# A two-layer decoder trunk on one core: more products inside the opening's five steps, and eight weight tiles kept back at the end

## The chip, the core and the metric

The kernel runs on one core of a Trainium2 chip. The metric is device time in microseconds of one execution; the number for a kernel is the median of its runs. The engines are named as in the profile: PE is TensorE's matmuls and PEld its weight loads, DVE is VectorE, ACT is ScalarE, POOL is GpSimd, SP issues nearly all the DMAs.

## The reference

256 tokens of width 2048 go through two layers. Layer 0 mixes tokens with forgetting attention (16 heads of 128), layer 1 with sliding-window attention; each is followed by a gated feed-forward network with a short convolution. Every sub-layer is modulated by a conditioning vector `c`:

```python
def reference(x, c, positions, ...):
    c_act = jax.nn.silu(c)
    for i in range(DEPTH):
        mod = c_act @ ada_w[i] + ada_b[i]
        sh1, sc1, g1, sh2, sc2, g2 = jnp.split(mod[:, None, :], 6, axis=-1)
        h = x * (1.0 + sc1) + sh1
        ...
        y = fox_attention(h, fox_w_in[j], fox_b_f[j], fox_w_o[j])      # layer 0; layer 1: swa_attention
        x = layer_norm(DEEPNORM_ALPHA * x + (1.0 + g1) * y, ln_mix_g[i], ln_mix_b[i])
        h = x * (1.0 + sc2) + sh2
        y = conv_ffn(h, ffn_w_up[i], ffn_conv_w[i], ffn_conv_b[i], ffn_w_down[i])
        x = layer_norm(DEEPNORM_ALPHA * x + (1.0 + g2) * y, ln_ffn_g[i], ln_ffn_b[i])
    return x
```

All is in float32. So `h`, the input of the very first projection (2048 to 6144 columns for queries, keys and values), needs the shift `sh1` and the scale `1 + sc1` first, which are products of `c` with 33.5 MB of `ada_w`.

## The kernel before

**Products in three parts.** A float32 product is made of float32r products: every operand is split into a high half (`h`, `hH`, a cast on ACT) and a low half (`l`, `hL`, the rest, a subtraction on DVE), and three matmuls add high x high, high x low and low x high in PSUM.

**Units.** `stream` (line 260) fetches weights in tiles of 256 rows x 512 columns (512 KB), which are called units here. For each, SP issues a DMA into one of ten `w` buffers (line 265), ACT makes `wh` (line 268), DVE makes `wl` (line 279), and PE does 24 matmuls over 256 columns (`w_mm`, weights stationary) or 12 over 512 columns (`x_mm`, activations stationary). `wh` and `wl` have four buffers each. The whole kernel has 728 units. Work is kept in a list and emitted up to two units behind the fetches (`then`, `settle`, `rest`); the low half of a unit is emitted ahead of the unit's products.

**The opening** (`opening`, line 535) works on `sh1` and `sc1` in five steps, because 2048 columns of each come in pieces of 256, 256, 512, 512 and 512. In a step, pieces of `ada_w` (`wo`) arrive, DVE adds them up weighted by `c` (line 576, one sum for each 512 KB or less), a few matmuls of one column sum over the partitions (`products`, `totals`, tile `cps`), and the columns of `hH` and `hL` that the step makes known are written by `mod_pair`. With these the projection can begin before the rest of `h` exists: a list `plan` (line 898) says which units are done while each following step's pieces arrive. An entry `(blk, k2)` stands for three units (queries, keys and values of a block of four heads) at rows `256 * k2` to `256 * k2 + 255`. The first list is empty, and the sixth is what follows the steps. At the end of each step two units of the next list are emitted ahead of the step's transposes.

Four blocks of heads exist. A block that is not finished within the opening leaves partial sums in PSUM, which `keep` copies with ACT to SBUF (line 919; two tiles of 128x512 each for queries, keys and values), as the eight PSUM banks are wanted by the next. Some go to the four quarters of the tile `gate`, the others to tiles of the pool `gp`. Later, when the rest of the block's units is done, `evac_qk` (line 847) and `evac_v` (line 834) add them in with DVE (lines 852 and 838). Once the block whose sums lie in `gate` has read them, `gate_free` is set.

**After the opening** the blocks are finished in the order 0, 2, 1, 3: first what is left of the units of queries, keys and values of a block, then its four heads (scores, softmax, output) as background generators that advance with each unit. `out_proj` (line 750) multiplies the heads' outputs with `w_o`, 32 units: the first two column blocks go over heads 0 to 7, then 8 to 11, then 12 to 15, the other two over all at once. Each column block ends with a residual addition and statistics for the layer norm on DVE (`residual`, line 629).

**The modulation of what follows** is streamed beside this. `ada_vector` (line 373) makes one of the other modulation vectors: 32 tiles `wa` of 512 KB and for each a sum on DVE (lines 395 and 397), then a few more generator steps. How fast it goes is set by hand: `ada["rate"]` is the number of generator steps per unit, 1.6 for the rest of the opening's list, then 1.6, 1.6, 1.5 and 1.4 for the four blocks, then 1.3 in the output projection. Three vectors (119 steps, 96 sums) have to be ready by the end of the output projection. The sums and many other DVE instructions are kept in program order; the rest is ordered when the program is built.

**The end.** The feed-forward network of layer 1 ends with the down-projection's second part, ten units for each of four column blocks (`x_stationary`, line 323). For the last column block `x_mm_end` (line 298) does the last four units in two passes: first the products of token tile 0 of all four, then those of token tile 1. Token tile 0's chain (residual, statistics, the layer norm at lines 1180 and 1181, the output's DMAs) can so begin while PE does the second pass. The `wh` and `wl` of the units kept this way stay occupied until then.

Of the kernel before, what the change touches and what calls it, by code (L numbers as in the profile page):

```python
# [41 lines left out]
def hybrid_trunk(ctx: ExitStack, tc: tile.TileContext, a: dict, out: bass.AP):  # L42
# [217 lines left out]
    def stream(wsrc, row0, col, ks, use):  # L260

        for kc in ks[::2]:
            r0 = (row0 + kc) * P
            w = wtile()
            pin(nc.sync.dma_start(w, wsrc[r0:r0 + 2 * P, col:col + WB].rearrange("(k p) f -> p k f", p=P)), False)
            h = hl.tile([P, 2, WB], F32R, tag="wh", name="wh")
            l = hl.tile([P, 2, WB], F32R, tag="wl", name="wl")
            pin(nc.scalar.copy(h, w), False)  # L268

            def go(kc=kc, h=h, l=l):  # L270
                ahead[0] -= 1
                run_post()
                use(kc, h, l)
                if feeds:
                    feeds.pop(0)()
                tick()

            def residual_(w=w, h=h, l=l, go=go):
                pin(nc.vector.tensor_tensor(l, w, f32(h), op=ALU.subtract), behind[0] > 0)  # L279
# [470 lines left out]
    def out_proj(oT, full, w_o, l):  # L750
# [26 lines left out]
    def fox(l, j):  # L777
# [56 lines left out]
        def evac_v(ps, V, then, old):  # L834
# [8 lines left out]
            if old and old is next(iter(olds.values()))[2]:  # L843
                ada["gate_free"] = True
# [17 lines left out]
        def head(blk, hh, q, k, V):  # L862
# [22 lines left out]
            def outputs(pT):  # L885
# [15 lines left out]
        last = {}  # L901
        for items in plan:
            for blk, k2 in items:
                last[blk] = 2 * k2 + 1

        final = plan[-1][-1][0]

        def keep(blk, part):

            ps = banks[blk][part]  # L910
            if not old and part == 0:
# [3 lines left out]
                ada["gate_free"] = False  # L915
            g = [room.pop(0) if room else f32(gtile("part")).rearrange("p a b -> p (a b)") for _ in range(2)]
            old.setdefault(blk, []).append(g)
            for gi, pi in zip(g, ps):
                pin(nc.scalar.copy(gi, pi if part == 2 else pi.rearrange("p a s -> p (a s)")))
# [3 lines left out]
        def first_block(blk, k2, part):  # L923
            ps = banks.setdefault(blk, [None] * 3)
            k = 2 * k2
            if not done.get((blk, part)):
                then(lambda: ps.__setitem__(part, (w_banks, w_banks, x_banks)[part]()))

            def use(kc, h, l):
                if part < 2:  # L930
                    w_mm(ps[part], kc, h, l, last[blk])
                else:
                    x_mm(ps[part], kc, h, l, hstat, last[blk])
# [3 lines left out]
            if blk != final and k + 1 == last[blk]:  # L937
                then(lambda: keep(blk, part))
# [4 lines left out]
        for blk, rate in zip((0, 2, 1, 3), (1.6, 1.6, 1.5, 1.4)):  # L943
# [4 lines left out]
            def more(part, banks_, mul):  # L948
                if n == KC:
                    return banks[blk][part]  # L950
# [135 lines left out]
    def conv_ffn(l):  # L1086
# [37 lines left out]
        for si, (b0, b1) in enumerate(sbs):  # L1124
# [21 lines left out]
            for d in range(D // WB):  # L1146
                ps = x_stationary(w_dn, d * WB, b0 * 4, (b1 - b0) * 4, stat, (2, 4)[l] if si > 0 and d == D // WB - 1 else 0)
# [61 lines left out]
```

## Time and profile before

| | before |
|---|---|
| median of 3 runs | 2212.91 us (2211.6 to 2215.46) |
| the profiled execution | 2215.89 us, span 2214.0 us |
| units | 728 |
| units in the opening's five steps | 39, and 6 after them |
| last matmul of the kernel starts | 2199.79 us |
| last DVE instruction starts | 2208.82 us (a pair, 1.41 us) |

The prediction quotes views of one profiled execution. Times are microseconds from the span's start. A row of groups gives the line of the code, the engine, the operation, the tiles out<-in with their shapes, the count, then the busy time, the mean of one in nanoseconds, and the idle time before them. A row of waits gives who waited for whom, the sum, the number of waits and the longest. A row of windows gives the stretch and its length, the busy time and number of instructions of each engine, the granted clock of TensorE (1.00 is full), the DMA engines' share and what they moved. A row of the timeline gives start, duration, engine, line and instruction, with the idle time before it and what ended that in square brackets.

### The profile page before, as it was taken

To read this page: it belongs to the slowest core of one execution; us is meant where nothing else is said; L and a number is where in the kernel's file an instruction comes from. 1 tells how busy PE (TensorE), PEld (TensorE's weight loads), DVE (VectorE), ACT (ScalarE), POOL (GpSimd) and SP (SyncE) were. 2 spreads that over 40 slices of the span, in tenths; PEclk is the share of its full clock that TensorE was granted. 3 is DMA by queue.
4 is the path that set the end of the run, shared out by engine and by line. 5 is a ranking of instruction groups with operands and counts; after the bars stand their busy time and mean duration, and the time that the engine had idled before them with its cause. 6 is when DMAs were issued, how large, how long until landed. Compare 5 with 4: busy or idle time off the path is not lost. (4 is left out here: it accounts for less than half of the span.)

```text
span 2214.0 us, 38357 instructions
## 1 busy us (share of the span) xinstructions
PE 2164.3 (98%) x14915; PEld 1976.7 (89%) x14915; DVE 1792.8 (81%) x2459; ACT 1159.6 (52%) x1841; POOL 19.0 (1%) x48
## 2 busy tenths in 40 slices
PE   6999999999999999999999999999999999999997
PEld 5999888789999988999987877789999988999986
DVE  6879998989978979799798888789888655666756
ACT  3435656465565543655644677555555533555532
POOL 0000000000000000000000000000000000000000
PEclk9999999999999999999999999999999999999999
DMA  9999998979978989899797676678888566666663
GB/s 334 368 352 366 351 352 298 327 257 323 349 234 300 322 312 385 260 311 322 251 354 290 201 240 206 208 257 295 281 264 270 187 194 195 192 195 195 191 195 108
DMA packets 274246, 602.98 MB, mean 272 GB/s; under 512 B 21062, under 2 KB 29960, under 8 KB 273552
## 3 DMA queue, kind: packets, MB, share of 16 engines
q1 hardware_dynamic: 273008, 595.85, 79.6%
q0 software_dynamic: 1056, 4.69, 0.6%
q8 instruction: 116, 1.90, 0.3%
q14 instruction: 66, 0.54, 0.1%
HBM read 598.37 MB, written 2.10 MB: 271 GB/s over the span
## 5 line engine op out<-in xcount | busy, mean ns | idle before, releaser
L268 ACT CAST wh<-w 128x1024 fp32r<-128x1024 f32 x728 | 765.3, 1053 | 790.0 <-PE ws L75 284.5
L75 PE MATMUL ws<-hH,wh 128*128 128x256 f32 x6656 | 1153.3, 278 | 4.6 <-ACT hH L84 2.1
L279 DVE TENSOR_TENSOR wl<-w,wh 128x1024 fp32r<-128x1024 f32 x728 | 887.6, 1222 | 325.3 <-ACT wh L268 308.5
L75 PEld LDWEIGHTS ws<-hH,wh 128*128 128x128 f32 x6656 | 1012.1, 189 | 9.0 <-ACT hH L84 2.3
L75 PE MATMUL ws<-hH,wl 128*128 128x256 f32 x3328 | 918.6, 277 | 4.3 <-DVE wl L279 4.0
L75 PEld LDWEIGHTS ws<-hH,wl 128*128 128x128 f32 x3328 | 628.5, 189 | 6.0 <-DVE wl L279 5.9
L75 PE MATMUL xs<-wh,gT 128*128 128x512 f32 x1408 | 435.3, 389 | 0.0
L75 PEld LDWEIGHTS xs<-wh,gT 128*128 128x128 f32 x1408 | 264.3, 188 | 54.7
L75 PE MATMUL xs<-wl,gT 128*128 128x512 f32 x704 | 273.9, 389 | 0.0
L75 PE MATMUL xs<-wh,hH 128*128 128x512 f32 x704 | 235.9, 401 | 0.0
L397 DVE SCALAR_TENSOR_TENSOR acc<-wa,cact,acc 128x1024 f32<-128x1024 f32 x180 | 228.4, 1278 | 0.0
L397 DVE SCALAR_TENSOR_TENSOR acc<-wa,cactp,acc 128x1024 f32<-128x1024 f32 x128 | 162.3, 1278 | 0.3 <-DMA acc<-in_ada_b_dram 0.3
L75 PEld LDWEIGHTS xs<-wh,hH 128*128 128x128 f32 x704 | 131.3, 188 | 29.4 <-issue 0.7
L75 PEld LDWEIGHTS xs<-wl,gT 128*128 128x128 f32 x704 | 132.2, 188 | 27.4
L75 PE MATMUL xs<-wl,hH 128*128 128x512 f32 x352 | 138.7, 395 | 2.5 <-DVE wl L279 2.5
L1093 ACT ACTIVATE u<-ws,ccol 128x256 f32<-128x256 f32 x176 | 96.7, 562 | 58.5 <-PE ws L75 43.3
L75 PE MATMUL xs<-wh,oT 128*128 128x512 f32 x384 | 126.2, 397 | 0.8 <-ACT oT L84 0.8
L1094 DVE SCALAR_TENSOR_TENSOR u<-ws,ccol,u 128x255 f32<-128x255 f32 x176 | 82.6, 477 | 14.9 <-ACT u L1093 14.7
L75 PEld LDWEIGHTS xs<-wh,oT 128*128 128x128 f32 x384 | 72.1, 188 | 16.6 <-ACT oT L84 1.2
L1096 DVE SCALAR_TENSOR_TENSOR u<-ws,ccol,u 128x254 f32<-128x254 f32 x176 | 83.1, 477 | 2.2
L75 PEld LDWEIGHTS xs<-wl,hH 128*128 128x128 f32 x352 | 66.5, 189 | 17.5 <-DVE wl L279 4.3
L576 DVE SCALAR_TENSOR_TENSOR oacc<-wo,cact,oacc 128x1024 f32<-128x1024 f32 (+1 forms) x68 | 73.3, 1078 | 8.3 <-DMA wo<-in_ada_w_dram 7.1
(220 smaller groups left out, 1280.4 us busy)
## 6 DMA issues: line engine op xcount, KB each, us to landing
w<-in_ffn_w_up_dram SPq DMA_DIRECT2D x352, 512.0 KB, 4.7
wa<-in_ada_w_dram SPq DMA_DIRECT2D x320, 512.0 KB, 5.6
w<-in_ffn_w_down_dram SPq DMA_DIRECT2D x176, 512.0 KB, 4.9
w<-in_fox_w_in_dram SPq DMA_DIRECT2D x96, 512.0 KB, 6.9
wo<-in_ada_w_dram SPq DMA_DIRECT2D x48, 512.0 KB, 9.0
w<-in_swa_w_in_dram SPq DMA_DIRECT2D x40, 512.0 KB, 4.6
w<-in_fox_w_o_dram SPq DMA_DIRECT2D x32, 512.0 KB, 6.2
w<-in_swa_w_o_dram SPq DMA_DIRECT2D x32, 512.0 KB, 4.8
```

The source lines that it names most:

```text
L75: return nc.tensor.matmul(o, lhsT, rhs, start=start, stop=stop, **kw)
L268: pin(nc.scalar.copy(h, w), False)
L279: pin(nc.vector.tensor_tensor(l, w, f32(h), op=ALU.subtract), behind[0] > 0)
L397: pin(nc.vector.scalar_tensor_tensor(ac, wo, (cactp if row else cact)[:, k:k + 1], ac, op0=ALU.mult, op1=ALU.add), True)
L576: nc.vector.scalar_tensor_tensor(acc, w[:, k], cact[:, kc:kc + 1], acc, op0=ALU.mult, op1=ALU.add)
L1093: nc.scalar.activation(u, pf, AF.Identity, bias=cw(CW, f), scale=cw(2, f))
L1094: nc.vector.scalar_tensor_tensor(u[:, 1:], pf[:, :S - 1], cw(1, f), u[:, 1:], op0=ALU.mult, op1=ALU.add)
L1096: nc.vector.scalar_tensor_tensor(u[:, 2:], pf[:, :S - 2], cw(0, f), u[:, 2:], op0=ALU.mult, op1=ALU.add)
```

## The change

Three things are changed.

1. The plan. Before, the block visits in the opening were 2 (one entry), 1 (two), 3 (four), 0 (eight). Now they are 3 (one), 1 (two), 2 (four), 3 again (five), 0 (eight). The units in the five steps go from 0 + 6 + 9 + 12 + 12 = 39 to 0 + 6 + 9 + 15 + 18 = 48, and those after them from 6 to 12. `keep` is called for four visits of three parts; where a block already has partial sums, DVE adds the PSUM tile to them instead of ACT copying it. The gate tile's quarters go to block 1, which is the first whose sums are read.
2. The rest of the blocks is finished in the order 0, 1, 2, 3, with 0, 18, 12 and 6 units left (before, for 0, 2, 1, 3: 0, 21, 18 and 12). The rates of ada steps are 1.6, 1.6, 1.6 and 1.5 for the blocks and 1.5 in layer 0's output projection.
3. The last column block of layer 1's down-projection keeps eight units instead of four for the second pass. The first four of these have `wh` and `wl` in the space of `hH` and `hL`, whose last use is past, the other four in the four buffers.

```diff
-    def stream(wsrc, row0, col, ks, use):
+    def stream(wsrc, row0, col, ks, use, spare={}):
...
-            h = hl.tile([P, 2, WB], F32R, tag="wh", name="wh")
-            l = hl.tile([P, 2, WB], F32R, tag="wl", name="wl")
+            h, l = spare.get(kc) or (hl.tile([P, 2, WB], F32R, tag=n, name=n) for n in ("wh", "wl"))
...
+    def spares(nk):
+        t = [hpad[:, 56 + i * 2 * WB:56 + (i + 1) * 2 * WB].rearrange("p (a f) -> p a f", a=2) for i in range(8)]
+        return {nk - 16 + 2 * i: (t[2 * i], t[2 * i + 1]) for i in range(4)}
...
-        stream(wsrc, k0, col, list(range(nk)), use)
+        stream(wsrc, k0, col, list(range(nk)), use, spares(nk) if end == 8 else {})
...
-            then(lambda i=i: ada.update(rate=(1.3, 0.65)[l]))
+            then(lambda i=i: ada.update(rate=(1.5, 0.65)[l]))
...
-        then(lambda: (ada_need(l, 2), ada.update(rate=(1.3, 0.75)[l])))
+        then(lambda: (ada_need(l, 2), ada.update(rate=(1.5, 0.75)[l])))
...
-            if old and old is next(iter(olds.values()))[2]:
+            if old and old is olds[1][2]:
                 ada["gate_free"] = True
...
-        plan = [[], [(2, 0), (1, 0)], [(1, 1), (3, 0), (3, 1)], [(3, 2), (3, 3), (0, 0), (0, 1)],
-                [(0, 2), (0, 3), (0, 4), (0, 5)], [(0, 6), (0, 7)]]
+        plan = [[], [(3, 0), (1, 0)], [(1, 1), (2, 0), (2, 1)], [(2, 2), (2, 3), (3, 1), (3, 2), (3, 3)],
+                [(3, 4), (3, 5), (0, 0), (0, 1), (0, 2), (0, 3)], [(0, 4), (0, 5), (0, 6), (0, 7)]]
...
+        visits = []
         for items in plan:
             for blk, k2 in items:
-                last[blk] = 2 * k2 + 1
+                if not visits or visits[-1][0] != blk:
+                    visits.append((blk, []))
+                visits[-1][1].append(k2)
+        visit = {(blk, k2): (n, 2 * ks[0], 2 * ks[-1] + 1) for n, (blk, ks) in enumerate(visits) for k2 in ks}
+        first_read = 1
...
+            parts = old.setdefault(blk, [])
+            flat = [pi if part == 2 else pi.rearrange("p a s -> p (a s)") for pi in ps]
+            if part < len(parts):
+                for gi, pi in zip(parts[part], flat):
+                    nc.vector.tensor_tensor(gi, pi, gi, op=ALU.add)
+                return
             g = [room.pop(0) if room else f32(gtile("part")).rearrange("p a b -> p (a b)") for _ in range(2)]
-            old.setdefault(blk, []).append(g)
-            for gi, pi in zip(g, ps):
-                pin(nc.scalar.copy(gi, pi if part == 2 else pi.rearrange("p a s -> p (a s)")))
+            parts.append(g)
+            for gi, pi in zip(g, flat):
+                pin(nc.scalar.copy(gi, pi))
...
-            if blk != final and k + 1 == last[blk]:
-                then(lambda: keep(blk, part))
+            if k + 1 == v1:
+                if v1 < KC - 1:
+                    then(lambda: keep(blk, part, ps[part]))
+                else:
+                    banks[blk, part] = ps
...
-        for blk, rate in zip((0, 2, 1, 3), (1.6, 1.6, 1.5, 1.4)):
+        for blk, rate in zip((0, 1, 2, 3), (1.6, 1.6, 1.6, 1.5)):
...
-                ps = x_stationary(w_dn, d * WB, b0 * 4, (b1 - b0) * 4, stat, (2, 4)[l] if si > 0 and d == D // WB - 1 else 0)
+                ps = x_stationary(w_dn, d * WB, b0 * 4, (b1 - b0) * 4, stat, (2, 8)[l] if si > 0 and d == D // WB - 1 else 0)
```

More of the change, by code (lines that the diff above doesn't have):

```diff
@@ L896, in fox, with keep @@
         TC = KC // 2
-        plan = [[], [(2, 0), (1, 0)], [(1, 1), (3, 0), (3, 1)], [(3, 2), (3, 3), (0, 0), (0, 1)],
-                [(0, 2), (0, 3), (0, 4), (0, 5)], [(0, 6), (0, 7)]]
+        plan = [[], [(3, 0), (1, 0)], [(1, 1), (2, 0), (2, 1)], [(2, 2), (2, 3), (3, 1), (3, 2), (3, 3)],
+                [(3, 4), (3, 5), (0, 0), (0, 1), (0, 2), (0, 3)], [(0, 4), (0, 5), (0, 6), (0, 7)]]
         done, banks, old = {}, {}, olds
-        last = {}
+        visits = []
         for items in plan:
             for blk, k2 in items:
-                last[blk] = 2 * k2 + 1
[L906 to L911, printed above, removed]
+                if not visits or visits[-1][0] != blk:
[3 more added lines that the diff above has]
+        first_read = 1
+        def keep(blk, part, ps):
+            if blk == first_read and part == 0:
                 gt = cst.tile([P, D], F32, tag="gate", name="gpart")
@@ L915, in keep @@
                 ada["gate_free"] = False
+            parts = old.setdefault(blk, [])
[4 more added lines that the diff above has]
+                return
             g = [room.pop(0) if room else f32(gtile("part")).rearrange("p a b -> p (a b)") for _ in range(2)]
[L917 to L919 removed]
+            parts.append(g)
+            for gi, pi in zip(g, flat):
+                pin(nc.scalar.copy(gi, pi))
         room = []
         def first_block(blk, k2, part):
[L924 removed]
+            n, v0, v1 = visit[blk, k2]
+            ps = banks.setdefault(n, [None] * 3)
             k = 2 * k2
[L926 removed]
+            if k == v0:
                 then(lambda: ps.__setitem__(part, (w_banks, w_banks, x_banks)[part]()))
@@ L946, in fox, with more @@
             n = done.get((blk, 0), 0)
-            def more(part, banks_, mul):
+            def more(part, banks_, mul, n=n, blk=blk):
                 if n == KC:
-                    return banks[blk][part]
+                    return banks[blk, part][part]
                 ps = banks_()
```

4 lines of the change are left out of this document (2 added, 2 removed).

## The prediction

> **What bounds the kernel now.** I read the page first, for the engines' shares.
>
> ```profile
> span 2214.0 us, 38357 instructions
> PE 2164.3 (98%) x14915; PEld 1976.7 (89%) x14915; DVE 1792.8 (81%) x2459; ACT 1159.6 (52%) x1841; POOL 19.0 (1%) x48
> ```
>
> PE (TensorE) is busy almost throughout, so only places where it waits can give time back. Next comes the view of windows, from step 3 of the opening up to the last unit of the output projection. A unit is one 512 KB weight tile with its products: 24 matmuls over 256 columns or 12 over 512. The windows begin where the timeline, with matmuls counted, shows a unit's first one. Columns: window, its length, busy us (instructions) of PE, PEld, DVE, ACT, POOL, clock, DMA share, GB/s.
>
> ```profile
> 86.90:126.50 39.60, 39.60 (x279) 37.24 (x278) 34.02 (x34) 17.89 (x23) 0.00 (x0) 0.94 1.02 364
> 126.50:170.00 43.50, 42.93 (x298) 39.50 (x297) 35.40 (x36) 15.23 (x17) 2.58 (x5) 0.96 0.99 337
> 170.00:187.60 17.60, 16.92 (x122) 15.42 (x120) 15.21 (x19) 9.45 (x16) 0.00 (x0) 1.00 1.03 396
> 187.60:265.70 78.10, 75.82 (x556) 70.20 (x557) 73.83 (x117) 51.80 (x109) 5.84 (x12) 1.00 0.99 347
> 265.70:324.10 58.40, 57.56 (x422) 53.71 (x421) 57.32 (x75) 31.66 (x59) 0.00 (x0) 1.00 0.98 359
> 324.10:369.60 45.50, 42.74 (x301) 38.80 (x300) 39.42 (x59) 28.82 (x56) 0.00 (x0) 1.00 0.87 309
> 369.60:410.20 40.60, 40.60 (x208) 34.37 (x206) 39.33 (x55) 23.85 (x49) 0.00 (x0) 1.00 0.98 355
> 410.20:468.30 58.10, 56.37 (x255) 45.34 (x253) 48.81 (x56) 25.61 (x55) 0.55 (x1) 1.00 0.92 325
> ```
>
> The first two rows are about steps 3 and 4 of the opening: PE is full, DMA near its limit, DVE (VectorE) has a seventh free. From 187.6 on (heads blocks 2, 1, 3, then two rows of output projection) PE and DVE are both nearly full. The view of waits gives what PE waited for: first in 57 to 170, then (three rows) in 170 to 468.
>
> ```profile
> PE xs L75 <- DVE wl L279: 0.6, 1, 0.6
> ```
> ```profile
> PE xs L75 <- DVE wl L279: 3.7, 3, 1.7
> PE ws L75 <- DVE wl L279: 3.3, 4, 1.4
> PE ws L75 <- ACT wh L268: 0.7, 1, 0.7
> ```
>
> So the long opening steps hold 0.6 us of waiting, and what follows holds 7.7 us, nearly all for DVE's low halves. That is the whole stake there: the change moves units out of a stretch where PE and DVE tie into one where PE alone is the bound.
>
> **The change part by part.** *Opening.* Steps 1 and 2 keep 6 and 9 units; step 3 goes from 12 to 15, step 4 from 12 to 18: nine more. What a unit takes there, and later:
>
> ```profile
> L75 PE MATMUL ws<-hH,wh 128*128 128x256 f32 x96 | 16.6, 277 | 0.0
> L75 PE MATMUL xs<-wh,hH 128*128 128x512 f32 x17 | 5.8, 397 | 0.0
> ```
> ```profile
> 2183.89 1.05 ACT L268 CAST wh<-w 128x1024 fp32r<-128x1024 f32 x1 [1.67 <-PE xs L75]
> 2186.61 1.05 ACT L268 CAST wh<-w 128x1024 fp32r<-128x1024 f32 x1 [1.67 <-PE xs L75]
> ```
>
> The first two rows are groups in the window 90.30 to 112.51: 16 such matmuls a unit make six units, 8 make two, so 22.21 / 8 = 2.78 us. The casts, each freed by PE's finished unit, stand 2.72 apart. So the opening grows by 9 x 2.78 = **+25.0**, and the later blocks shrink by 9 x 2.72 = **-24.5**. The total of products, casts, DMAs and SP's issues is unchanged: SP issues the same tiles, nine of them earlier. Step 3's and 4's denser mix gives DVE more PE time per ada row, so I let the 0.6 us wait go: **-0.6**; next late there is PE itself.
>
> *Keeping partial sums.* Four visits instead of three. The second visit of block 3 adds with DVE where a first visit copies with ACT:
>
> ```profile
> L919 ACT COPY part<-ws x8: 580/589/591, 61.0 to 106.3; 128x512 f32<-128x512 f32 x8
> L852 DVE TENSOR_TENSOR sum<-ws,part x8: 668/682/694, 285.3 to 355.1; 128x512 f32<-128x512 f32 x8
> ACT part L919 <- PE ws L75: 5.6, 3, 4.2
> ```
>
> Copies stay at 18 (three first visits, six each); added are six adds of 0.68 (the same kind of add), 4.1 us. Step 4 then has 35.4 + 6 x 1.14 + 4.1 = 46.3 us of DVE in 43.5 + 6 x 2.78 = 60.2, so PE hides them: 0. Without that cover they cost 4.1. They are also waits on PE in DVE's queue, behind which low halves stand; the third row has ACT's copies waiting up to 4.2 us for PE in 60 to 170. [...]
>
> *The ends of the steps* keep their one-column matmuls, after which the clock drops. Windows around the ends of steps 2 and 3:
>
> ```profile
> 78.70:86.90 8.20, 8.20 (x53) 8.20 (x51) 3.63 (x5) 1.74 (x3) 0.00 (x0) 0.65 0.99 359
> 118.10:129.80 11.70, 11.70 (x79) 11.06 (x78) 5.44 (x8) 4.33 (x5) 0.00 (x0) 0.85 1.04 382
> ```
>
> Lost clock is 8.2 x 0.35 = 2.9 us and 11.7 x 0.15 = 1.8. The ends of steps 3 and 4 shift, so each can move by 1.1 either way: 0, with 2.2 for the range. [...]
>
> *After the opening* I compare DVE's load with the time left. ada rows (the streamed modulation rows, one DVE sum each) come at a rate per unit; 96 have to be done, and the generator's steps put 36, 38, 22 of them into the units up to the end of block 1, up to the output projection's twelfth unit, and after it. Before, the same three stretches (170 to 265.7, to 410.2, to 468.3) have 32, 51, 13:
>
> ```profile
> L397 DVE SCALAR_TENSOR_TENSOR acc<-wa,cact,acc 128x1024 f32<-128x1024 f32 x30 | 37.5, 1277 | 0.0
> L395 DVE TENSOR_SCALAR acc<-wa,cact 128x1024 f32<-128x1024 f32 x2 | 1.5, 748 | 0.0
> ```
> ```profile
> L397 DVE SCALAR_TENSOR_TENSOR acc<-wa,cactp,acc 128x1024 f32<-128x1024 f32 x32 | 40.1, 1278 | 0.3 <-DMA acc<-in_ada_b_dram 0.3
> L397 DVE SCALAR_TENSOR_TENSOR acc<-wa,cact,acc 128x1024 f32<-128x1024 f32 x17 | 21.5, 1278 | 0.0
> L395 DVE TENSOR_SCALAR acc<-wa,cact 128x1024 f32<-128x1024 f32 x2 | 1.5, 752 | 0.0
> ...
> L397 DVE SCALAR_TENSOR_TENSOR acc<-wa,cact,acc 128x1024 f32<-128x1024 f32 x13 | 16.2, 1275 | 0.0
> ```
>
> Back to back they follow closer than they last:
>
> ```profile
> 434.16 3.66 DVE L397 SCALAR_TENSOR_TENSOR acc<-wa,cact,acc 128x1024 f32<-128x1024 f32 x3
> 437.74 1.22 DVE L279 TENSOR_TENSOR wl<-w,wh 128x1024 fp32r<-128x1024 f32 x1
> ...
> 448.26 2.35 DVE L279 TENSOR_TENSOR wl<-w,wh 128x1024 fp32r<-128x1024 f32 x2
> 450.54 0.68 DVE L632 TENSOR_TENSOR t<-xs,gate 128x512 f32<-128x512 f32 x1
> ```
>
> 3.58 / 3 = 1.19 a sum, 2.28 / 2 = 1.14 a low half. First stretch: 3 more units and 4 more sums, 89.0 + 3.4 + 4.8 = 97.2 us of DVE in 95.7 + 8.2 = 103.9; idle 6.7 as before: 0. Second: 12 units and 13 sums fewer, 136.1 - 13.7 - 15.5 = 106.9 in 144.5 - 32.6 = 111.9; idle 5.0 where it was 8.4. If DVE still needs 8.4, +3.4; I take **+0.5**, as its densest row (57.32 of 58.40) idles 1.1. Third: the same 20 units, 9 sums more, 48.8 + 10.7 = 59.5 in 58.1: DVE becomes the bound, at least +1.4, and +10.7 if it idles its 9.3 us as before. I take **+1.4**: this window shows DVE can run full,
>
> ```profile
> 416.00:459.00 43.00, 41.27 (x187) 33.18 (x187) 42.40 (x51) 19.79 (x46) 0.55 (x1) 1.00 0.90 307
> ```
>
> 42.40 of 43.00, and most idle time lies after 459, where the sums are over. On the other side the 7.7 us of waits can go. The gate's tile is free after block 1 (step 45 of the rows), before the second vector wants it (step 73), and all 119 steps fit into the 121 that the rates give: no cost; two steps short would cost two sums, 2.4. The blocks' new order is free too: the output projection's first eight slices want heads of blocks 0 and 1, now done sooner, and block 2's heads have 6 units of block 3 and 8 of the projection, where block 3's had 12 before without a PE wait for them in the rows above.
>
> *The end.* With four units kept, the first token tile's chain (timeline of DVE at the end) starts here and is still running when PE ends:
>
> ```profile
> 2194.78 0.69 DVE L632 TENSOR_TENSOR t<-xs,gate 128x512 f32<-128x512 f32 x1 [3.13 <-PE xs L75]
> ...
> 2208.82 1.41 DVE L1181 SCALAR_TENSOR_TENSOR x<-x,rs,ln 128x512 f32<-128x512 f32 x2
> ```
>
> PE's last matmul is this:
>
> ```profile
> 2199.79 0.39 PE L75 MATMUL xs<-wh,gT 128*128 128x512 f32 x1
> ```
>
> Both chains are 2194.78 to 2210.23, 15.45 us without a gap, so 7.7 each. PE ends at 2200.2; 10.0 of DVE follow. Half a unit, one token tile, is 2.72 / 2 = 1.36; eight kept units start the first chain 4 x 1.36 = 5.4 us earlier; it is over before PE ends and 7.7 remain: **-2.3**, and more kept units could not give more. The output's DMAs follow as before. The kept pass needs a unit each 1.36 us; a cast is 1.05 and a low half 1.14, and four pairs lie in room that the up-projection last read 30 units before, so they can run ahead. If they can't: 0.
>
> Sum: 25.0 - 24.5 - 0.6 + 0.5 + 1.4 - 2.3 = **-0.5**. The profiled execution took 2215.89 (span 2214.0), 3.0 above the median 2212.91; it becomes 2215.4, and by the median **2212.4**.
>
> **The rivals.** *A, PE's waits vanish* (faster): the longer steps 3 and 4 leave DVE (46.3 of 60.2) and DMA room, so both enter the blocks ahead; the added 1.9 does not come and 5 of the 7.7 go: -0.5 - 1.9 - 5.0 = -7.4, 2205.5. For it: fewer sums in the second stretch. Against it: DVE's load per PE time rises in all three.
> *B, VectorE bounds the output projection* (slower): its second part gets 22 sums for 13, three residuals among them, and low halves come late; decisive once DVE lags by the four buffered units. It keeps 9.3 us idle: +10.7 for +1.4, so +8.8, 2221.7. For it: 59.5 in 58.1, and nine tiles (4.7 MB) more beside 325 GB/s. Against it: the full window above.
> *C, adds block DVE's queue*: one full wait of 4.2 reaches PE: +3.7, 2216.6. Against it: DVE is loosest just there.
> *D, the end does not shorten*, the casts keeping PE's old pace: +1.8, 2214.7. Against it: free room for four pairs.
>
> **How the numbers follow.** Forecast 0.40, A 0.27, B 0.20, C 0.07, D 0.06. 0.2% is 4.4 us, about what a measurement of this kernel can tell from no change. A is faster, B slower; forecast, C and D lie within, but terms of the range (clock 2.2, second stretch 3.4, waits) put 0.06 of the forecast beyond on the faster side and 0.05 on the slower: faster 0.33, same 0.42, slower 0.25. The range reaches to A and B with part of the clock's term at A: 2204 to 2222.
>
> **What would show it.** Right: the last one-column group of the opening about 25 us later; block rows that together shrink by 24 to 25; DVE above 0.97 of the output projection's second part; a DVE gap ahead of the last residual and 7.7 us behind PE's end. Wrong: PE waits for low halves well over 7.7 (B) or under 3 (A); PE waiting at block 3's second visit (C); the second tile's chain still mixed with the first's (D). A step 3 or 4 that grows by less than 2.78 a unit would mean that PE was not its bound.

## The result, and the profile after

| | before | changed |
|---|---|---|
| median | 2214.18 us (2211.6 to 2215.75, 8 runs) | 2221.75 us (2218.14 to 2224.57, 8 runs) |
| the profiled execution | 2215.89 us, span 2214.0 | 2224.28 us, span 2222.2 |

The ratio is 1.0034, 95% interval 1.0025 to 1.0043: the change makes the kernel slower by a third of a per cent, where the forecast was 0.5 us faster. Counts and shares of the engines, from the page of the changed kernel:

```profile
span 2222.2 us, 38352 instructions
PE 2168.5 (98%) x14915; PEld 1978.1 (89%) x14915; DVE 1794.5 (81%) x2465; ACT 1157.5 (52%) x1841; POOL 19.0 (1%) x48
```

The work is the same but for the six adds on DVE (2465 for 2459), and the shares tell nothing. So the stages have to be laid beside one another. Next is the view of windows of the changed kernel, columns as in the prediction. The first two rows are steps 3 and 4, the next two the ten units behind the steps that end block 0 and then block 1; blocks 2 and 3 follow, and the output projection in two parts, 12 and 19 units.

```profile
87.30:136.50 49.20, 49.20 (x340) 46.27 (x339) 36.59 (x35) 20.30 (x24) 0.00 (x0) 0.93 1.02 370
136.50:192.70 56.20, 56.20 (x404) 52.71 (x402) 43.44 (x45) 20.91 (x22) 2.58 (x5) 0.97 0.96 313
192.70:229.70 37.00, 34.11 (x244) 30.95 (x241) 31.63 (x35) 16.20 (x23) 0.00 (x0) 1.00 0.92 338
229.70:303.70 74.00, 69.19 (x496) 64.91 (x497) 65.22 (x110) 47.73 (x105) 5.82 (x12) 0.95 0.91 311
303.70:346.30 42.60, 39.91 (x291) 36.40 (x290) 42.49 (x60) 23.17 (x47) 0.00 (x0) 1.00 0.99 366
346.30:367.10 20.80, 20.50 (x148) 18.78 (x149) 20.80 (x25) 9.86 (x15) 0.00 (x0) 1.00 0.95 330
367.10:416.30 49.20, 48.31 (x251) 39.70 (x249) 43.42 (x83) 38.66 (x90) 0.00 (x0) 1.00 0.84 286
416.30:478.80 62.50, 59.12 (x255) 46.33 (x254) 59.16 (x65) 25.10 (x55) 0.54 (x1) 0.97 0.95 340
```

Beside the rows of before, stretch by stretch ("due" is before's time with the moved units at 2.72 us each, in the first row with the 24.4 us that were forecast):

| stretch | before | due | after | difference | forecast |
|---|---|---|---|---|---|
| up to the end of step 4 | 170.0 | 194.4 | 192.7 | -1.7 | 0 (24.4 due) |
| first, to the end of block 1 | 95.7 | 103.9 | 111.0 | **+7.1** | 0 |
| second, to the projection's 12th unit | 144.5 | 111.9 | 112.6 | +0.7 | +0.5 |
| third, the next 19 units | 58.1 | 58.1 | 62.5 | **+4.4** | +1.4 |
| DVE after PE's last matmul | 10.05 | 10.05 | 7.97 | -2.1 | -2.3 |

Due are -0.1 in all (24.4 - 24.5); with the differences that makes 8.3. The spans differ by 8.2: what lies between the third stretch and PE's end takes 1731.9 us before and 1731.6 in the changed kernel. So two stretches carry the loss, both behind the part of the opening that was lengthened.

**The first stretch.** The window around the end of the ten units, in pieces of 5 us:

```profile
215.00:220.00 5.00, 5.00 (x33) 4.43 (x33) 3.65 (x4) 0.00 (x0) 0.00 (x0) 1.00 1.03 404
220.00:225.00 5.00, 4.06 (x33) 3.54 (x31) 2.02 (x3) 2.13 (x3) 0.00 (x0) 1.00 1.05 397
225.00:230.00 5.00, 3.05 (x13) 2.13 (x13) 5.00 (x6) 2.90 (x5) 0.00 (x0) 1.00 0.99 357
230.00:235.00 5.00, 2.17 (x12) 1.96 (x11) 5.00 (x5) 2.44 (x3) 0.00 (x0) 0.72 1.01 371
235.00:240.00 5.00, 5.00 (x29) 5.00 (x29) 2.05 (x3) 0.17 (x1) 0.00 (x0) 0.60 0.94 360
```

First, before PE has lost anything, the DMA engines are full (share 1.03 to 1.05) at about 400 GB/s and ACT does nothing from 215 to 220. Then PE is short of work from 220 to 235, and the granted clock falls. Ten units with 16 ada tiles are 26 tiles of 512 KB, 13.6 MB. At PE's pace they are wanted in 33.4 us (the time of the ten units in quiet10 and reuse10 below, where PE doesn't wait), which is 408 GB/s, where the engines moved 404 and 397 in the first two rows. The queue of SP shows when and in which order tiles are asked for:

```profile
188.67 0.33 SPq L394 DMA_DIRECT2D wa<-in_ada_w_dram  x1
196.07 0.38 SPq L265 DMA_DIRECT2D w<-in_fox_w_in_dram  x1
...
208.09 0.38 SPq L265 DMA_DIRECT2D w<-in_fox_w_in_dram  x1
209.29 4.99 SPq L394 DMA_DIRECT2D wa<-in_ada_w_dram  x5
215.15 2.72 SPq L265 DMA_DIRECT2D w<-in_fox_w_in_dram  x3
```

Between the first two rows SP waits 7.0 us for a buffer, until DVE has split the forget gate's weights (`fl`), and from 195 to 200 the engines move 142 GB/s; before has the same wait (5.6 us), with six units behind it. So the engines are not full over the whole stretch, and with a demand above the 404 and 397 nothing is left to make that up. The third row is the weight of the last of the ten units. It lands at 217.4, and five ada tiles go out before the next weight. What ACT does meanwhile (timeline of ACT, changed kernel):

```profile
220.08 0.60 ACT L858 ACTIVATE qh<-ws 128x512 fp32r<-128x512 f32 x1 [5.40 <-PE ws L75]
222.80 0.59 ACT L84 CAST qh<-ws 128x512 fp32r<-128x512 f32 x1 [2.12 <-PE ws L75]
223.28 1.05 ACT L267 CAST wh<-w 128x1024 fp32r<-128x1024 f32 x1
...
228.54 3.90 ACT L267 CAST wh<-w 128x1024 fp32r<-128x1024 f32 x4
```

A weight that landed at 217.4 is cast at 223.28, behind two copies of block 0's results that each wait for PE; four later weights are cast at 228.54 in one run. Their low halves come later still, behind two ada sums (timeline of DVE, changed kernel):

```profile
229.70 2.46 DVE L400 SCALAR_TENSOR_TENSOR acc<-wa,cact,acc 128x1024 f32<-128x1024 f32 x2
232.09 3.48 DVE L278 TENSOR_TENSOR wl<-w,wh 128x1024 fp32r<-128x1024 f32 x3
```

PE waits four times meanwhile, 0.94, 0.53, 1.42 and 2.83 us. In before, the corresponding cast stands ahead of those copies (same view, before):

```profile
175.66 1.05 ACT L268 CAST wh<-w 128x1024 fp32r<-128x1024 f32 x1 [0.20 <-PE ws L75]
...
180.72 0.60 ACT L855 ACTIVATE qh<-ws 128x512 fp32r<-128x512 f32 x1 [4.01 <-PE ws L75]
```

**The third stretch.** DVE is busy 59.16 of 62.50 us there, and low halves stand behind other work of DVE (timeline of DVE, then what PE waited for, changed kernel):

```profile
441.69 3.65 DVE L400 SCALAR_TENSOR_TENSOR acc<-wa,cact,acc 128x1024 f32<-128x1024 f32 x3
445.27 1.22 DVE L278 TENSOR_TENSOR wl<-w,wh 128x1024 fp32r<-128x1024 f32 x1
```
```profile
PE xs L75 <- DVE wl L278: 3.1, 3, 2.3
```

The longest wait, 2.3 us, ends at 446.54 with the low half that stands behind three sums; the other two (0.30 and 0.46 us) end with low halves among the residual's instructions. Behind the longest the granted clock is at half for 3.4 us, which is 1.7 of the 4.4 us.

**The end.** DVE at the end of the changed kernel (timeline); PE's last matmul starts at 2210.01 and takes 0.39:

```profile
2210.44 0.69 DVE L635 TENSOR_TENSOR t<-xs,gate 128x512 f32<-128x512 f32 x1 [2.94 <-PE xs L75]
...
2216.96 1.41 DVE L1196 SCALAR_TENSOR_TENSOR x<-x,rs,ln 128x512 f32<-128x512 f32 x2
```

DVE waits 2.94 us ahead of the second residual, so the first chain is over in time; from 2210.40 to 2218.37 only one chain, 7.97 us, follows PE.

### The profile page after: what moved, and what is told of

It reads as the page before. It is cut to its first block, busy times and chain, and to the rows that moved or that the text cites. A ratio compares the mean times of both kernels' runs of the same rounds, so it can differ in the third digit from the quotient of the medians.

```text
span 2222.2 us, 38352 instructions
## 1 busy us (share of the span) xinstructions
PE 2168.5 (98%) x14915; PEld 1978.1 (89%) x14915; DVE 1794.5 (81%) x2465; ACT 1157.5 (52%) x1841; POOL 19.0 (1%) x48
## 4 chain that ended last, share of the span: by engine, by line
PE 70%; DVE 5%; ACT 2%; issue 1%; DMA 0%; DVEq 0%; POOL 0%; ACTq 0%
PE ws L75 42%; PE xs L75 27%; DVE wl L278 1%; DVE acc L400 1%; ACT wh L267 1%; DVE pr L708 1%; PE sm L499 0%; ACT pr L1074 0%; ACT pr L712 0%; PE sm L442 0%; PE sm L75 0%; DVE x L680 0%; DVE x L681 0%; PE spin L75 0%; DVE qL L85 0%
## 5 line engine op out<-in xcount | busy, mean ns | idle before, releaser
L75 PE MATMUL xs<-wh,gT 128*128 128x512 f32 x1376 | 425.8, 389 | 0.0
L75 PEld LDWEIGHTS xs<-wh,gT 128*128 128x128 f32 x1376 | 258.3, 188 | 53.7
L75 PE MATMUL xs<-wl,gT 128*128 128x512 f32 x688 | 267.7, 389 | 0.0
L75 PEld LDWEIGHTS xs<-wh,oT 128*128 128x128 f32 x384 | 72.5, 189 | 16.3 <-DVE oT L85 0.5
```

The costliest lines, as they stand in the source:

```text
L75: return nc.tensor.matmul(o, lhsT, rhs, start=start, stop=stop, **kw)
```

## The experiments

**My theories for the first stretch.** Theory 1: the DMA engines are asked for more in the ten units than they move; a weight lands late, stands behind copies in ACT's order, and the casts behind them come late too. Theory 2 (rival): ACT's order alone does it, also with weights that land in time. Theory 3 (rival): DVE's sums in this stretch hold up the low halves. For the third stretch: DVE is the bound (theory), or the nine further tiles are (rival). Each series had its own runs of before beside it, with medians 2213.81, 2213.61 and 2212.68 us, and lateorder 2213.26.

**tail8**: before, with the eight units kept at the end alone (`spares` as in the change).

```diff
-... (2, 4)[l] if si > 0 and d == D // WB - 1 else 0)
+... (2, 8)[l] if si > 0 and d == D // WB - 1 else 0)
```

> The kernel before with only the eight kept units at the end; plan, order and rates as before. The prediction's term for the end is -2.3 us, and the changed kernel's trace shows 7.9 us of VectorE behind the last matmul instead of 10.0. If this part stands alone: 2.0 to 2.3 us faster than before (ratio 0.9990). If the end gains nothing by itself: equal to before.

2212.6 us (11 runs), ratio 0.9993, 0.9984 to 1.0001; run again in the third series as **tail8_b**:

> The kernel before with eight kept units at the end alone, once more beside the other two: its first series gave 0.9993 of before (0.9984 to 1.0001), its trace 2 us less behind the last matmul. 1.5 to 2.3 us faster than before if the end's gain is real.

2210.64 us (11 runs), 0.9989, 0.998 to 0.9997. In its profile DVE waits 2.95 us ahead of the last residual, as in the changed kernel. By the medians this part gives 1.2 and 2.0 us by itself; the second time the interval excludes no change.

**open48**: the changed kernel with four units kept, so the opening, the order and the rates alone.

```diff
-... (2, 8)[l] ...
+... (2, 4)[l] ...
```

> The changed kernel with four kept units at the end, so the new plan, order and rates alone. If the two parts add up, it is 2 us slower than the changed kernel, 9 to 10 us slower than before (ratio 1.0043). If the loss came from the end, it equals before.

2226.85 us by five runs, 1.0056, 1.0041 to 1.0071; a sixth took 6680.23 us, three times the others, which isn't explained. The loss is here. It stands 0.0022 above the whole change's 1.0034; the end's 2 us are 0.0009 of that, and the rest is within the two intervals.

**rising**: before, with blocks 1 and 2 exchanged in plan and order.

```diff
-        plan = [[], [(2, 0), (1, 0)], [(1, 1), (3, 0), (3, 1)], ...
+        plan = [[], [(1, 0), (2, 0)], [(2, 1), (3, 0), (3, 1)], ...
-        for blk, rate in zip((0, 2, 1, 3), (1.6, 1.6, 1.5, 1.4)):
+        for blk, rate in zip((0, 1, 2, 3), (1.6, 1.6, 1.5, 1.4)):
```

> The kernel before with blocks 1 and 2 exchanged in the plan, so that blocks are finished in the order 0, 1, 2, 3; 39 units in the five steps, three visits, rates and end as before. The prediction took the order to be free: equal to before within 0.1%. If block 2's heads come too late for the output projection: slower by 1 us or more, with a wait at its units 8 to 12.

2212.93 us (10 runs), 0.9998, 0.999 to 1.0007. The order is free, as the prediction had it.

**quiet10**: the changed kernel with half the ada steps in the ten units, and more of them in the output projection's first part.

```diff
-                then(lambda: ada.update(rate=1.6))
+                then(lambda: ada.update(rate=0.8))
-            then(lambda i=i: ada.update(rate=(1.5, 0.65)[l]))
+            then(lambda i=i: ada.update(rate=(2.2, 0.65)[l]))
```

> The changed kernel with 0.8 ada steps a unit instead of 1.6 in the ten units that follow the opening's steps, and 2.2 instead of 1.5 in the output projection's first twelve units, so that all 119 steps still fit. Theory 1 (weights come too late there: ten units with 16 ada tiles are 26 tiles of 512 KB in 28 us, more than the DMA engines move, so unit 59's cast misses its place ahead of block 0's evacuation on ScalarE): the 9 us that units 57 to 60 lose go, 2214 to 2216 us. Theory 2 (ScalarE stands at block 0's evacuation whatever the ada rows do, because twelve units are left there): equal to the changed kernel within 2 us. Theory 3 (VectorE is overfull there with the sums): as theory 1; the next kernel tells 1 from 3.

2224.33 us (6 runs), 1.0044, 1.0028 to 1.006. Its rows for the ten units, the rest of block 1, and the two parts of the output projection:

```profile
187.40:220.80 33.40, 33.40 (x243) 31.11 (x242) 25.58 (x27) 15.88 (x21) 0.00 (x0) 1.00 0.95 339
...
353.70:410.40 56.70, 51.32 (x249) 41.55 (x248) 51.01 (x89) 39.21 (x90) 0.00 (x0) 0.94 0.86 297
```

The stall is gone: 33.4 us for 37.0, 103.1 for 111.0 with the rest of block 1. But the kernel is not at the 2214 to 2216 us expected: with the sums that were put off the first part of the projection takes 56.7 for 49.2 us, 3.4 of that by the clock (0.06 of 56.70), and the gain is spent. This takes both tiles and sums from the ten units, so it doesn't part theory 1 from 3; the next one does.

**reuse10**: in the stretch with the ten units every second ada tile isn't loaded; its sum is done on the tile before.

```diff
-                w = wtile("wa").rearrange("p a f -> p (a f)")
-                pin(nc.sync.dma_start(w, ...), False)
+                if not (c and ada.get("reuse")):
+                    w = wtile("wa").rearrange("p a f -> p (a f)")
+                    pin(nc.sync.dma_start(w, ...), False)
...
-                then(lambda: ada.update(rate=1.6))
+                then(lambda: ada.update(rate=1.6, reuse=True))
```

> The changed kernel with every second ada tile of those ten units not loaded: the sum takes the tile before a second time, so the modulation comes out wrong, VectorE does the same 16 sums and the DMA engines move 8 tiles fewer. Theory 1: units 57 to 60 lose at most 2 us instead of 9, the kernel is 5 to 8 us faster than the changed one, 2214 to 2217. Theories 2 and 3: the loss at units 57 to 60 stays, equal to the changed kernel within 2 us.

2216.3 us (12 runs), 1.0007, 0.9996 to 1.0018, against 1.0034 for the change. Windows of the ten units and the rest of block 1:

```profile
187.00:220.40 33.40, 33.40 (x243) 31.14 (x242) 32.34 (x34) 16.08 (x20) 0.00 (x0) 1.00 0.92 313
220.40:290.90 70.50, 67.84 (x496) 63.84 (x495) 64.22 (x111) 48.48 (x107) 5.84 (x12) 0.98 0.91 304
```

33.4 + 70.5 = 103.9, what was due to the tenth, with DVE's sums all there (32.34 of 33.40 busy, more densely than in the changed kernel's 31.63 of 37.00). So theory 3 falls. The last weight of the ten lands at 205.1 and is wanted by PE at 217.60. But ACT's order differs as well: in this program its cast (214.90) stands behind only the first of the copies (214.40), and the next weights' casts ahead of the second (221.58); so transfers and order changed together, and 1 and 2 aren't parted yet. The next two runs take one of them each.

**castfirst**: the changed kernel with some 15 casts and block 0's copies on ACT held in program order, so that copies don't pass ahead of a cast.

```diff
-            pin(nc.scalar.copy(h, w), False)
+            units[0] += 1
+            pin(nc.scalar.copy(h, w), 50 <= units[0] <= 64)
...
-                    nc.scalar.copy(v, ps[t])
+                    pin(nc.scalar.copy(v, ps[t]), not old)
```

> The changed kernel with the order of ScalarE written out at the handover: the casts of fifteen units from unit 49 or 50 on and block 0's own copies out of PSUM stay in the order in which the program names them, so unit 59's and 60's casts stand ahead of block 0's copies. Theory 1 (weights land late because the DMA engines are full; unit 59's landed at 217.4 while ScalarE already stood at block 0's first copy until 220.1, so its cast began at 223.3): the cast of unit 59 starts when its weight lands and its wait goes; units 60 and later still want weights that land late, so 2 to 6 us come back, units 48 to 78 in 105 to 109 us instead of 111. If lateness alone counted and the copies did not: no change. If the order alone counted: all 7 come back.

2218.65 us (12 runs), 1.0022, 1.0011 to 1.0032. The ten units take 34.2 us and the rest 71.0 (rows of the windows, then of ACT):

```profile
186.60:220.80 34.20, 33.60 (x243) 30.95 (x241) 32.21 (x33) 13.58 (x17) 0.00 (x0) 1.00 0.96 354
220.80:291.80 71.00, 68.38 (x496) 63.97 (x497) 64.24 (x110) 50.79 (x110) 5.85 (x12) 0.98 0.95 337
```
```profile
219.74 1.05 ACT L269 CAST wh<-w 128x1024 fp32r<-128x1024 f32 x1 [6.73 <-DMA w<-in_fox_w_in_dram]
...
223.34 0.59 ACT L860 ACTIVATE qh<-ws 128x512 fp32r<-128x512 f32 x1
```

The weights still come late (ACT waits 6.73 us for one), but each is cast as it lands and the copies go after it: 105.2 us in all, 5.8 of the 7.1 are back. By the medians less comes back, 1.0022 against 1.0034, with intervals that overlap. But nine of castfirst's twelve runs had a mean clock of 0.993 or less, and only four of the changed kernel's eight (last section). At 0.994 or 0.995 its three runs took 2211.73 to 2213.09 us, the changed kernel's four 2218.14 to 2219.7.

**lateorder**: reuse10 with the order of the changed kernel on ACT: the casts of the last of the ten units and of the next one wait for PE through a small copy.

```diff
+    def hold_cast(src):
+        settle()
+        pin(nc.scalar.copy(cst.tile([P, 8], F32, tag="held", name="held"), src))
+        hold["on"] = True
...
-            pin(nc.scalar.copy(h, w), False)
+            pin(nc.scalar.copy(h, w), hold["on"])
+            hold["on"] = False
...
+            if (blk, k2, part) == (0, TC - 1, 2):
+                hold_cast(ps[1][0][:, 0, 0:8])
...
-        settle()
+        hold_cast(banks[0, 2][2][0][:, 0:8])
```

> As the run with every second ada tile left out in the ten units (so its sums there use the tile before, and part of the modulation is computed from wrong rows), but the cast of the last of the ten units has to wait for PE's 59th unit, and the next cast for the 60th, through a copy of eight columns that ScalarE makes ahead of each: the order that ScalarE has in the changed kernel, with weights that land in time. If the order alone makes the stall (transfers in time don't help), the ten units and the rest of block 1 take 109 to 112 us again, PE waits near unit 60 for about 3 to 5 us, and the kernel is at 2220 to 2223. If the late transfer itself makes it (theory 1 as I read it), they take 104 as in the run without the hold, and the kernel is at 2215 to 2217.

2272.16 us (5 runs), 1.0264, 1.025 to 1.0278: far from both expectations, for a reason outside the stretch (last section). The stretch itself can be read; ACT first, then the two windows:

```profile
224.14 0.17 ACT L264 COPY held<-ws 128x8 f32<-128x8 f32 x1 [2.28 <-PE ws L75]
224.21 1.05 ACT L274 CAST wh<-w 128x1024 fp32r<-128x1024 f32 x1
228.08 0.17 ACT L264 COPY held<-xs 128x8 f32<-128x8 f32 x1 [2.83 <-PE xs L75]
228.16 2.95 ACT L274 CAST wh<-w 128x1024 fp32r<-128x1024 f32 x3
```
```profile
193.20:229.30 36.10, 34.97 (x244) 31.95 (x242) 32.53 (x34) 14.40 (x21) 0.00 (x0) 1.00 0.86 295
229.30:298.60 69.30, 67.73 (x495) 63.79 (x496) 63.06 (x110) 49.90 (x109) 5.87 (x12) 1.00 0.89 299
```

The casts come as late as in the changed kernel, after PE's 59th and 60th unit, though their weights had landed at 212.5 and 214.9. The stretch takes 105.4 us, 1.5 more than reuse10, and part of that is that its matmuls are slower. Free of the clock in other places, though not of the slower matmuls, is the time between PE's first matmuls of the 59th and the 63rd unit, from the timelines:

| | weights late | weights in time |
|---|---|---|
| copies ahead of the casts | 25.9 us (changed kernel) | 19.0 (lateorder) |
| casts ahead of the copies | 18.6 (castfirst) | 17.1 (reuse10) |

Each alone costs 1.5 to 1.9 us, both together 8.8. Some 0.6 of lateorder's 1.9 is its slower matmuls (48 of them behind each other take 5.68 us from 237.90, the same 48 in the changed kernel 5.44 from 243.74; 120 lie in the interval). Of the 8.8, 5.7 are PE's four waits and 2.7 the half clock, at which 27 matmuls from 233.35 take 5.81 us, at a unit's full pace 3.06. The 8.8 is more than the 7.1 mostly because reuse10's 103.9 hold a drop of the clock later on: the row from 220.40 has 0.98 over 70.50 us, 1.4 us lost. So theory 2 falls as well, and theory 1 holds in its whole form only: the weights of the next units land at 225 to 228 *and* stand behind copies that wait for PE, so that four casts follow only at 228.54 and their low halves at 232.09. One thing is left open: the two sums at 229.70, 2.4 us ahead of these low halves, are already done in lateorder when its low halves are due, so DVE's order differs between the four kernels too, and no run changed it alone.

**out_thin** and **out_reuse**, for the third stretch: sums over 128 of the 1024 columns in the projection's last 20 units; and there every second ada tile not loaded, as in reuse10.

```diff
+                        if ada.get("thin"):
+                            ac, wo = ac[:, :P], wo[:, :P]
...
-        then(lambda: (ada_need(l, 2), ada.update(rate=(1.5, 0.75)[l])))
+        then(lambda: (ada_need(l, 2), ada.update(rate=(1.5, 0.75)[l], thin=l == 0)))
```

> The changed kernel, but in the last 20 units of layer 0's output projection each ada sum covers 128 of its 1024 columns, so the modulation is left incomplete; the tiles are loaded as before. There the stretch from unit 108 to 127 takes 62.5 us, before 58.2. Theory V (VectorE is the bound, 59.2 of 62.5 us busy): 22 sums lose about 1 us each, the stretch falls to 54 to 57 us and the kernel by 5 to 8 us against the changed one. Theory D (the nine tiles more make the DMA engines the bound, 0.95 of their time): the stretch stays at 61 to 63.

> The changed kernel, but in the same 20 units every second ada tile is not loaded and the sum takes the one before again, so the modulation is wrong; VectorE's work is the same. Theory V: unit 108 to 127 stays at 61 to 63 us. Theory D: it falls by 3 us or more, towards 58.

out_thin: 2215.64 us (10 runs), 1.0014, 1.0004 to 1.0024. out_reuse: 2222.96 (4 runs), 1.0043, 1.003 to 1.0056. The stretch in the one and in the other:

```profile
417.00:473.10 56.10, 56.08 (x256) 45.52 (x255) 39.24 (x62) 24.90 (x55) 0.55 (x1) 1.00 1.01 373
```
```profile
413.60:476.10 62.50, 59.63 (x255) 46.24 (x254) 59.17 (x65) 25.21 (x55) 0.55 (x1) 0.97 0.76 251
```

Shorter sums take 6.4 us from the stretch and PE has no idle time left; a DMA share of 0.76 for 0.95 takes nothing. VectorE is the bound there.

**spread10**: the changed kernel with rate 0.8 in the ten units, and the tiles that this puts off spread thinly over everything behind.

```diff
-                then(lambda: ada.update(rate=1.6))
+                then(lambda: ada.update(rate=0.8))
-        for blk, rate in zip((0, 1, 2, 3), (1.6, 1.6, 1.6, 1.5)):
+        for blk, rate in zip((0, 1, 2, 3), (1.75, 1.75, 1.75, 1.8)):
```

with 1.55 for 1.5 in the output projection.

> The changed kernel with 0.8 ada steps a unit in the ten units behind the opening's steps, and the eight steps saved there spread evenly: 1.75, 1.75, 1.75, 1.8 for the blocks and 1.55 in the output projection. quiet10 showed that the stall at units 57 to 60 goes (units 48 to 78 in 103 us instead of 111), but it gave 7.5 us back in the twelve units with a rate of 2.2. If the steps can be spread without a new bound: 7 us faster than the changed kernel, about 2215, equal to before. If VectorE is full in all that follows, as the sums per stretch say: it gives 3 to 6 us back, 2217 to 2220.

2222.18 us (6 runs), 1.0035, 1.0023 to 1.0047: a miss. Its windows for the ten units, block 3 and the projection's second part:

```profile
194.50:228.00 33.50, 33.50 (x244) 31.21 (x243) 25.63 (x28) 15.89 (x21) 0.00 (x0) 1.00 0.85 302
...
341.30:364.60 23.30, 20.70 (x147) 18.87 (x148) 23.30 (x28) 9.84 (x16) 0.00 (x0) 1.00 0.99 346
...
415.70:479.40 63.70, 58.31 (x255) 46.36 (x254) 60.15 (x64) 24.92 (x55) 0.55 (x1) 0.97 0.95 344
```

The stall is gone again (33.5 + 70.0 = 103.5 for 111.0), and 6.3 of the 7.5 us are given back: 0.7 in block 2, 23.3 - 20.8 = 2.5 in block 3, 1.9 and 63.7 - 62.5 = 1.2 in the projection. DVE is busy 23.30 of 23.30 and 60.15 of 63.70 us: block 3 has no room for a further sum, and the projection keeps about the idle time that it has in the changed kernel (3.55 and 3.34 us).

**mid45**: the changed kernel with 45 units in the steps and six behind them, so that the part behind the steps has before's size.

```diff
-... [(2, 2), (2, 3), (3, 1), (3, 2), (3, 3)],
-                [(3, 4), (3, 5), (0, 0), (0, 1), (0, 2), (0, 3)], [(0, 4), (0, 5), (0, 6), (0, 7)]]
+... [(2, 2), (2, 3), (3, 1), (3, 2), (0, 0)],
+                [(0, 1), (0, 2), (0, 3), (0, 4), (0, 5)], [(0, 6), (0, 7)]]
```

with rate 1.6 in all four blocks and 1.2 in the projection's last part.

> The changed kernel with 45 units in the five steps and 6 behind them as before: 15 in step 3, 15 in step 4, block 3's second visit has two entries; rates 1.6 for all four blocks, 1.5 for the output projection's first twelve units, 1.2 for its last twenty, 17 sums there instead of 22; eight kept units at the end. If the loss at the handover comes from ten units at a rate of 1.6 behind the steps: it is gone, units 42 to 78 lose no more than before's corresponding ones. VectorE's sums in the last twenty units: 1 to 3 us over before. With 2 us from the end: 2211 to 2215, equal to before or up to 0.15% faster. If it is the number of moved units that counts: two thirds of the changed kernel's loss, 2218 to 2220.

2216.12 us (12 runs), 1.002, 1.001 to 1.003: above what I expected. The six units behind the steps take 17.6 us, as in before. The 27 that end block 1, and the third stretch:

```profile
207.10:306.00 98.90, 95.51 (x735) 90.11 (x735) 94.91 (x145) 62.55 (x130) 5.87 (x12) 1.00 0.98 349
412.70:471.60 58.90, 57.12 (x256) 45.36 (x255) 54.32 (x60) 26.13 (x55) 0.55 (x1) 1.00 0.95 336
```

The stall behind the steps is gone and the third stretch is at 58.9, but the 27 units take 98.9 where before's 21 and six more would be 78.1 + 16.3 = 94.4. DVE is busy 94.91 of 98.90 there, a higher share than before's 73.83 of 78.10. What holds these 4.5 us wasn't told apart by a run; the longest wait of PE in them, 2.2 us, is for ACT's softmax tile `pr` and has no counterpart in before's 78.10.

## Why the prediction was wrong

By its own steps:

- *Opening, +25.0 - 0.6.* Right. Step 4 ends 22.7 us later; up to there the granted clock stood at half for 23.9 us in before and 20.5 in the changed kernel (windows of 1 us), which is 1.7 us of the difference; without it, +24.4. PE has no wait at all between 87 and 192.7, as the 0.6 demanded.
- *Adds on DVE, 0 (rival C).* Right: steps 3 and 4 have PE full in every window, DVE 36.59 of 49.20 and 43.44 of 56.20.
- *Clock, 0 with 2.2 either way.* -1.7, within, for the ends of the steps that the term was about. It left out drops behind the steps: from 170 to 480 us before's clock is full throughout, while the changed kernel's is at half for 6.8 us from 232 and for 3.4 us from 447, each time in or just behind a long wait of PE.
- *First stretch, "idle 6.7 as before: 0".* **The step that failed.** DVE's load was forecast at 97.2 us and is 31.63 + 65.22 = 96.85; but the idle time is 14.2 us and not 6.7. I compared DVE's load with the time over 30 units and took the other engines from before. What changed is inside: the short stretch behind the steps has ten units of its own pace and of ada tiles where it had six; 408 GB/s are wanted of engines that moved 397 to 404 at a share of 1.03 to 1.05, and 337 in the changed kernel's first 33.4 us; and what is buffered bridges six such units, as before's and mid45's 17.6 us show, but not ten. The rows of before showed it, had I asked: in 170.0 to 187.6 the DMA share is 1.03 at 396 GB/s, so that stretch was already full, and it got longer by two thirds. That would have been a warning and not yet the size. That this becomes a stall needs ACT's order too, which the argument did not look at: castfirst and lateorder each keep one half alone, which costs 1.5 to 1.9 us.
- *Second stretch, +0.5.* Right: +0.7.
- *Third stretch, +1.4.* The mechanism is right (DVE busy 59.16 us where 59.5 was forecast), the size was not: +4.4, because DVE still idles 3.3 us and PE loses 1.7 us to the half clock behind its longest wait, 2.3 us for a low half that stands behind three sums. B is thus half true: VectorE bounds the projection, but it keeps a third of its idle time, not all of it.
- *The end, -2.3.* Right: -2.1.
- *A* fell: DVE's load per PE time rose as the argument against A said, and PE's waits did not vanish but grew. *D* fell: the first chain is over in time in the changed kernel and in tail8.

By profiled times 2224.28 stands against 2215.4 forecast, 8.9 us: 7.1 of the first stretch, 3.0 of the third, 0.4 of the second and the end, less 1.7 of the clock. The medians add 0.5. The time is B's (2221.7), but that is luck: four fifths of the way there is by a mechanism that no case named.

Of all versions, before with the eight kept units (tail8) is the fastest, 0.9989 of before in the one series and 0.9993 in the other.

## What to carry to other kernels

When units are moved, compare demand with supply for each engine, the DMA engines too, over the shortest stretch that has a pace of its own, not over the sum of stretches: here what was buffered carried six units, and ten were too many. Look in an engine's timeline which instructions stand ahead of the one that feeds PE: here two copies on ACT, which waited 5.40 and 2.12 us for PE's results ahead of a cast that PE's next unit needed, turned a transfer that was a little late into a stall, while each of the two alone cost 1.5 to 1.9 us. And before work is put off to a later stretch, ask what is the bound there; here the sums that quiet10 and spread10 took out of the ten units gained 7.9 and 7.5 us, and cost 7.5 and 6.3 in the stretches that took them.

## What the runs showed of the hardware

The granted clock at the ends of the opening's steps differs between executions of the same code. Windows around the ends of steps 2 and 3, in the profile of the changed kernel and then in that of reuse10, whose code is the same up to there:

```profile
78.00:88.00 10.00, 10.00 (x63) 9.26 (x64) 7.05 (x11) 4.69 (x7) 0.00 (x0) 0.83 1.05 385
118.00:132.00 14.00, 14.00 (x89) 13.43 (x89) 5.09 (x7) 3.61 (x4) 0.00 (x0) 0.80 0.96 336
```
```profile
78.00:88.00 10.00, 10.00 (x73) 9.01 (x73) 6.88 (x10) 3.98 (x7) 0.00 (x0) 1.00 1.04 385
118.00:132.00 14.00, 14.00 (x104) 13.10 (x103) 6.29 (x9) 4.38 (x6) 0.00 (x0) 1.00 1.01 350
```

The lost clock is 1.7 + 2.8 = 4.5 us in the one, nothing in the other. It also shows in the eight runs of the changed kernel: four took 2223.8 to 2224.57 us at a mean clock of 0.991 or 0.992, four 2218.14 to 2219.7 at 0.994. So two executions of this kernel differed by up to 6.4 us with nothing changed, about as much as the loss that was looked for; that is why stretches were compared here with their clock beside them, and versions by the intervals of their ratios.

Behind PE's longer waits the clock fell in some cases only. In the changed kernel it went to half for 3.4 us, 0.7 us behind the end of a wait of 2.31 us (446.54; windows of 0.1 us). The row of reuse10 from 220.40, with a wait of 2.4 us, has a clock of 0.98, and so has castfirst's from 220.80, with one of 1.8; the row of mid45 from 207.10 holds a wait of 2.2 us at a clock of 1.00. So in the changed kernel 1.7 us of lost clock came on top of the 2.31, and the length of a wait alone doesn't tell whether the clock falls.

With a tile of eight columns more, the whole kernel was slower. In lateorder PE is slower at full clock also where nothing was changed: from the output projection's last matmul on `oT` to PE's last matmul it takes 1787.0 us, in reuse10 1734.3. The view of groups from 1704 to 2104 us, lateorder and then reuse10:

```profile
L75 PE MATMUL ws<-hH,wh 128*128 128x256 f32 x1489 | 268.2, 282 | 0.0
```
```profile
L75 PE MATMUL ws<-hH,wh 128*128 128x256 f32 x1476 | 251.3, 275 | 0.0
```

Each matmul over 256 columns takes 282 for 275 ns by its row, and the casts of such units follow each other at 2.88 us (1959.57 and 1962.45) for 2.72 (1902.62 and 1905.34); matmuls over 512 columns are unchanged at 389 ns. What the runs differ in, beside the stretch, is the tile `held` of 32 bytes in each partition, and that this tile is the cause, by moving the tiles placed after it, is argued, not shown: no run changed the placement alone.
